# Start-up loads, five small products of the recurrent stage and the last group's sums rearranged in a hybrid attention and RWKV-7 block

## The chip, the cores and the metric

The kernel runs on one core of one Trainium2 chip. The metric is the device time of one execution in microseconds; several runs are timed and their median is given. One further execution is recorded by the hardware profiler, and all views of the profile come from it.

## The reference

One layer over 2048 rows of 1024 features, all in float32:

```python
h    = rms_norm(x, pre_mix_g)
proj = h @ w_in                     # 1536 attention, 1792 recurrent, 2048 gate columns
q, k, v = split(proj[:, :1536])     # 8 heads of 64: own chunk of 64 rows + 8 chunks before,
y_a  = softmax(q k^T / 8 + bias[distance]) v
p    = proj[:, 1536:3328]
p    = p + (previous row of p - p) * shift_mu
r, k, v, cw, ca, cg = split(p)      # 512, 512, 512, 64, 64, 128
decay = exp(-exp(-softplus(-(w0 + tanh(cw) @ w2)) - 0.5)); a = sigmoid(a0 + ca @ a2)
# per head, over time: state = state*decay + (state @ -kk) (kk*a)^T + v k^T;  y = state @ r
y_b  = (group_norm(y) + sum(r*k*r_k) * v) * (sigmoid(cg) @ g2)
m    = sigmoid(gA) * (y_a @ proj_a) + sigmoid(gB) * (y_b @ proj_b)
x    = x + rms_norm(m @ w_out, post_mix_g)
x    = x + rms_norm(relu(rms_norm(x, pre_ffn_g) @ w_up)**2 @ w_down, post_ffn_g)
```

## The kernel before

**Groups and products.** The rows are worked in four groups of 512 (`G`), each through a recurrent phase (`phase_rwkv`), an attention phase and a merge (`phase_merge`); the feed-forward part follows for two halves of the rows. A dense product of h with 128 columns of `w_in` (`dense`) splits the weight block into a high part `whi` (ScalarE, L70) and a low rest `wlo` (VectorE, L71) and forms 24 products of 128x128 by 128x512 (L80): for each of eight blocks of h high by high, the low half of h (`hl`) by `whi`, and `hh` by `wlo`. The raw weight, `whi` and `wlo` have two buffers each. Loads of weights and rows go out on SP's queue, in the queue's order; stores and the sums' transfers mostly on POOL's, gates' stores on ScalarE's.

**The start.** `phase_norm` loads the gain and four tiles of 128 rows; `norm_tile` squares each (L319, ScalarE), forms its root on POOL (`rstd`, L105 and L107), scales it (`xn`, L321, VectorE) and transposes it in eight products (L126), each half of which ScalarE copies to `hh` (L130) and VectorE reduces to `hl` (L131). Two PSUM tiles serve these transposes. Then come the constants: ten loads of rows (L203), four of w2 and a2 (L210), a transpose (L212) and small VectorE operations, the bias band (`build_bias`: `ext` loaded, extended on VectorE, stored as `band` at L961, then eight copies of it into `skew` in DRAM, L963) and eight copies that spread a small unit matrix into `x0` (L229). After that the group's projections start: block 12 for the low-rank inputs (`lora_wa`), then r, k, v of the first pair of heads. The low-rank products ps_z and ps_a (L360, L361) stand behind the second projection.

**The recurrent phase.** Four pairs of heads are prepared by `rwkv_pre`, which calls `between()` at eight places to let a gate's dense product, or steps of another pair's recurrence, run in. In it stand ps_ss and ps_v, the bonus product in two parts (ps_bonus from `rh` and `rl`, L488), and the scores ps_A (L517) in two halves of 16 products on two PSUM tiles each. All these small products share a pool of two PSUM tiles (`pa`). `rwkv_inverse` inverts 32x32 triangles for two pairs at a time on VectorE (X, turned at L560 and L562); `rwkv_blocks` completes them to 64x64 by 64 products ps_t of the turned X (L582), a copy Z (L585), and 64 more (L590). Then follow the transposes and products of `rwkv_trans`, the serial recurrence over eight chunks (L665 to L668), and `rwkv_post` (squares of ps_y, root, yn at L686).

**What sets the order.** An engine works off its own queue in order. The queue's order is fixed when the kernel is built, not by the program's text alone: the trace shows later dense products between small ones. `queue_behind` adds an order without a wait on data; before, `blocks_behind` places the first and the second 64 block products behind the 4th and 13th, or the 12th and 21st, product of a dense group of 24.

**The last group's merge.** While `phase_merge` forms ps_o (L1070) in two halves of the output columns, one of the kernel's sums of weight blocks runs beside it: four loads into the tile `cmb`, four subtractions on VectorE (L1121), four stores to `wd` on POOL's queue (L1145). It advances one step at k = 2, 4, 5, 6, 7 of the first half. The first half's results are squared (L1080, ScalarE) and scaled (L1081, VectorE), which frees PSUM for the second half. The feed-forward part's first operand is loaded into `bl` and split (`first_half`, `split_here`, L1158 and L1159). Its memory is that of tiles released before, `cmb` among them.

Of the kernel before, what the change touches and what calls it, by code (L numbers as in the profile page):

```python
# [18 lines left out]
P = 128  # L19
D = 1024  # L20
# [14 lines left out]
STEPS = (1, 2, 1, 1, 1, 1, 1, 1, 1, 1, 1, 0, 0, 2, 1)  # L35
DEC = math.exp(-0.5)
# [14 lines left out]
class Block:  # L51
# [6 lines left out]
    def wsplit(self, src, tag, k, n, raw_tag="raw", bufs=2):  # L58

        nc = self.nc  # L60
        w = self.wp
        raw = w.tile([P, k, n], F32, tag=raw_tag, name="wraw")
        nc.sync.dma_start(raw, src)
        hi = w.tile([P, k, n], F32R, tag=tag + "h", bufs=bufs, name="whi")
        lo = w.tile([P, k, n], F32R, tag=tag + "l", bufs=bufs, name="wlo")
        self.split(hi, lo, raw)
        return hi, lo

    def split(self, hi, lo, src):
        high = self.nc.scalar.copy(hi, src)  # L70
        self.nc.vector.tensor_tensor(lo, src, hi.bitcast(F32), ALU.subtract)  # L71
        return high.ins

    def mm3(self, ps, terms):
# [3 lines left out]
        for lh, ll, rh, rl in terms:  # L78
            for l, r in ((lh, rh), (lh, rl), (ll, rh)):
                mm.append(nc.tensor.matmul(ps, l, r, start=n == 0, stop=n == last).ins)  # L80
                n += 1
# [6 lines left out]
    def blocks_behind(self, *places):  # L88

        for ins, i in zip(self.blocks, places):  # L90
            self.queue_behind(ins, self.mm[i])

    def dense(self, col):

        wh, wl = self.wsplit(
            self.a["w_in"][:, col : col + P].rearrange("(k p) n -> p k n", p=P), "w", KB, P
        )
        ps = self.pd.tile([P, G], F32, tag="d", name="psd")
        self.mm = self.mm3(ps, [(wh[:, k], wl[:, k], self.h[0][:, k], self.h[1][:, k]) for k in range(KB)])
        return ps  # L100

    def rstd(self, pool, ssq, scale, eps, post=None):
        nc = self.nc
        v = pool.tile([P, 1], F32, tag="rs_v", bufs=4, name="rs_v")
        nc.gpsimd.tensor_scalar(v, ssq, scale, eps, ALU.mult, ALU.add)  # L105
        r = pool.tile([P, 1], F32, tag="rs_r", bufs=4, name="rs_r")
        nc.gpsimd.tensor_tensor(r, v, self.nhalf[:, 0:1], ALU.pow)  # L107
# [11 lines left out]
    def transpose_split(self, pt, src, hi, lo, tok, pinned=False):  # L119

        nc = self.nc
        for h in range(2):
            ps = pt.tile([P, 4, P], F32, tag="tr", name="pstr")
            for j in range(4):
                k = h * 4 + j
                mm = nc.tensor.transpose(ps[:, j], src[:, k * P : (k + 1) * P], self.ident)  # L126
                if pinned and j == 0:
                    self.tc.keep_in_program_order(mm)
            hv, lv = hi[:, h * 4 : h * 4 + 4, tok], lo[:, h * 4 : h * 4 + 4, tok]
            nc.scalar.copy(hv, ps)  # L130
            nc.vector.tensor_tensor(lv, ps, hv.bitcast(F32), ALU.subtract)  # L131


    def constants(self, ctx, mixing):
# [57 lines left out]
        with tc.tile_pool(name="setup", bufs=1, side="right") as sp, \  # L192
# [19 lines left out]
            nc.tensor.transpose(ps, raw, self.ident[:nrow, :nrow])  # L212
            nc.vector.tensor_copy(self.cst, ps)

            for par in range(2):
# [4 lines left out]
                nc.vector.tensor_tensor(  # L220
                    self.wl[par][r], raw2[par][r], self.wh[par][r].bitcast(F32), ALU.subtract
                )
            self.build_bias(sp, dp)
# [4 lines left out]
            for i in range(8):  # L228
                nc.sync.dma_start(  # L229
                    self.x0[i * 16 : i * 16 + 16].rearrange("p r j -> p (r j)"),  # L230
                    eyed[i % 2][None, :].to_broadcast((16, 512)),
                )
# [52 lines left out]
    def phase_norm(self, g, sp, pt, ahead=2):  # L285

        self.h = self.alloc_h()
        gt = self.gain(sp, self.a["pre_mix_g"], "g_pre", ahead if ahead == 2 else 1)
        for t in range(GT):
            x = sp.tile([P, D], F32, tag="x", bufs=ahead, name="x")  # L290
            self.nc.sync.dma_start(x, self.a["x"][g * G + t * P : g * G + (t + 1) * P])
            self.norm_tile(sp, pt, x, gt, *self.h, slice(t * P, (t + 1) * P), ahead)
            yield
# [21 lines left out]
    def norm_tile(self, sp, pt, x, gt, hi, lo, tok, ahead=2, pinned=False):  # L315
# [3 lines left out]
        nc.scalar.activation(xn, x, AF.Square, accum_out=ssq)  # L319
        r = self.rstd(sp, ssq, 1.0 / D, RMS_EPS)  # L320
        nc.vector.scalar_tensor_tensor(xn, x, r, gt, op0=ALU.mult, op1=ALU.mult)  # L321
        self.transpose_split(pt, xn, hi, lo, tok, pinned)

# [53 lines left out]
    def rwkv_pre(self, g, p, rp, NA, between=lambda: None):  # L377
# [13 lines left out]
        if p == 3:  # L391
            self.blocks_behind(3, 12)
# [94 lines left out]
        for i, x in enumerate((rh, rl)):  # L487
            nc.tensor.matmul(psb, self.bones, x, start=i == 0, stop=i == 1)  # L488
# [1020 lines left out]
```

## Time and profile before

| | |
|---|---|
| median of 3 runs | 3300.28 us (3299.59 to 3302.99) |
| profiled execution | 3302.74 us, span in the trace 3301.0 us |
| TensorE busy | 3189.4 us, 97% of the span |
| VectorE, ScalarE, POOL busy | 68%, 48%, 18% |
| DMA | 592.53 MB, mean 179 GB/s |

The page's first section gives each engine's busy time. A line of the waits reads: engine and line that waited, what it waited for, microseconds in total, number of times, the longest. A line of a timeline reads: start and length in us, engine, line of the kernel, operation, the tile written and the tiles read, sizes, number of instructions merged, and in brackets the idle time just before with what ended it. A stretch is a line with its bounds and length, the busy time and number of instructions of TensorE, its weight loads, VectorE, ScalarE and POOL, then the granted clock of TensorE, the share of the DMA engines and GB/s.

### The profile page before, as it was taken

To read this page: it belongs to the slowest core of one execution; us is meant where nothing else is said; L and a number is where in the kernel's file an instruction comes from. 1 tells how busy PE (TensorE), PEld (TensorE's weight loads), DVE (VectorE), ACT (ScalarE), POOL (GpSimd) and SP (SyncE) were. 2 spreads that over 40 slices of the span, in tenths; PEclk is the share of its full clock that TensorE was granted. 3 is DMA by queue.
4 is the path that set the end of the run, shared out by engine and by line. 5 is a ranking of instruction groups with operands and counts; after the bars stand their busy time and mean duration, and the time that the engine had idled before them with its cause. 6 is when DMAs were issued, how large, how long until landed. Compare 5 with 4: busy or idle time off the path is not lost. (4 is left out here: it accounts for less than half of the span.)

```text
span 3301.0 us, 49967 instructions
## 1 busy us (share of the span) xinstructions
PE 3189.4 (97%) x18913; PEld 2601.3 (79%) x18913; DVE 2245.6 (68%) x3655; ACT 1570.8 (48%) x2511; POOL 595.8 (18%) x1093
## 2 busy tenths in 40 slices
PE   7999999999999999999999999999999999999998
PEld 5777778778877777878777887878788878888887
DVE  5875766785766875776876775777656667775455
ACT  3434634434744434754444654544543454454343
POOL 2222012222102222111232110122211112220000
PEclk9999999999999999999999999999999999999999
DMA  5335473247564236555326647654787875546665
GB/s 152 90 110 185 129 239 118 81 131 240 170 223 150 87 108 222 189 194 185 96 76 201 200 155 234 231 179 153 248 291 239 285 248 190 170 161 235 193 215 178
DMA packets 432281, 592.53 MB, mean 179 GB/s; under 512 B 25300, under 2 KB 295840, under 8 KB 432040
## 3 DMA queue, kind: packets, MB, share of 16 engines
q1 hardware_dynamic: 375080, 413.14, 40.0%
q0 software_dynamic: 47744, 159.42, 13.1%
q10 hardware_dynamic: 9216, 16.78, 1.4%
q8 instruction: 149, 2.44, 0.3%
q14 instruction: 92, 0.75, 0.1%
HBM read 425.37 MB, written 167.01 MB: 179 GB/s over the span
## 5 line engine op out<-in xcount | busy, mean ns | idle before, releaser
L1345 PE MATMUL ps_dn<-fop 128*128 128x512 f32 x2688 | 611.8, 389 | 2.9 <-DVE fop L71 2.9
L1345 PEld LDWEIGHTS ps_dn<-fop 128*128 128x128 f32 x2688 | 503.9, 188 | 108.9 <-DVE fop L71 4.3
L80 PE MATMUL psd<-hh,whi 128*128 128x512 f32 x1344 | 541.4, 403 | 10.7 <-ACT whi L70 7.0
L80 PE MATMUL psd<-hl,whi 128*128 128x512 f32 x1344 | 542.4, 404 | 0.0
L80 PE MATMUL psd<-hh,wlo 128*128 128x512 f32 x1344 | 538.5, 401 | 2.6 <-DVE wlo L71 2.6
L70 ACT CAST whi<-wraw 128x1024 fp32r<-128x1024 f32 x232 | 243.3, 1049 | 424.1 <-PE psd L80 329.9
L71 DVE TENSOR_TENSOR wlo<-wraw,whi 128x1024 fp32r<-128x1024 f32 x232 | 282.9, 1220 | 165.9 <-ACT whi L70 139.1
L80 PEld LDWEIGHTS psd<-hh,whi 128*128 128x128 f32 x1344 | 255.9, 190 | 62.1 <-ACT whi L70 7.9
L80 PEld LDWEIGHTS psd<-hh,wlo 128*128 128x128 f32 x1344 | 256.1, 191 | 55.9 <-DVE wlo L71 5.1
L80 PEld LDWEIGHTS psd<-hl,whi 128*128 128x128 f32 x1344 | 256.5, 191 | 48.9
L71 DVE TENSOR_TENSOR fop<-xraw,fop 128x1024 fp32r<-128x1024 f32 x112 | 137.0, 1223 | 166.7 <-ACT fop L70 165.9
L70 ACT CAST fop<-xraw 128x1024 fp32r<-128x1024 f32 x112 | 117.8, 1052 | 244.9 <-PE ps_dn L1345 178.5
L1227 POOL DMA_DIRECT2D xd<-X x192 | 103.8, 541 | 394.3 <-ACT X L1224 339.5
L71 DVE TENSOR_TENSOR fop<-wdraw,fop 128x1024 fp32r<-128x1024 f32 x112 | 136.6, 1220 | 26.6 <-ACT fop L70 26.1
L70 ACT CAST fop<-wdraw 128x1024 fp32r<-128x1024 f32 x112 | 117.7, 1051 | 42.8 <-DMA wdraw<-in_w_down_dram 29.8
L903 DVE CUSTOM_DVE_ANT_0 sc<-bias,ps_s 128x640 f32<-128x640 f32 (+4 forms) x128 | 93.8, 732 | 54.0 <-PE ps_pt L914 32.2
L908 ACT ACTIVATE sc<-sc,mn 128x640 f32<-128x640 f32 (+4 forms) x128 | 97.7, 764 | 45.2 <-DVE mn L903 44.8
L70 ACT CAST s12h<-s 128x1024 fp32r<-128x1024 f32 x32 | 33.7, 1054 | 165.0 <-PE ps_u L80 165.0
L80 PE MATMUL ps_p<-yh,whi 128*128 128x512 f32 x256 | 101.3, 405 | 7.5 <-DVE th L1041 3.8
L1070 PE MATMUL ps_o<-whi,mh 128*128 128x512 f32 x256 | 101.6, 397 | 6.1 <-DVE o L1081 6.1
L919 DVE TENSOR_TENSOR PTl<-ps_pt,PTh 128x640 fp32r<-128x640 f32 (+4 forms) x128 | 94.2, 736 | 18.7 <-ACT PTh L918 17.2
L1070 PE MATMUL ps_o<-wlo,mh 128*128 128x512 f32 x256 | 100.6, 393 | 3.2 <-DVE wlo L71 3.2
(368 smaller groups left out, 6826.1 us busy)
## 6 DMA issues: line engine op xcount, KB each, us to landing
wraw<-in_w_in_dram SPq DMA_DIRECT2D x168, 512.0 KB
xraw<-xd SPq DMA_DIRECT2D x112, 512.0 KB
xd<-X POOLq DMA_DIRECT2D x192, 256.0 KB, 5.2
wraw<-in_w_up_dram SPq DMA_DIRECT2D x80, 512.0 KB
wdraw<-wd SPq DMA_DIRECT2D x64, 512.0 KB
wdraw<-in_w_down_dram SPq DMA_DIRECT2D x48, 512.0 KB
gd<-gate ACTq DMA_DIRECT2D x64, 256.0 KB
wd<-cmb POOLq DMA_DIRECT2D x64, 256.0 KB, 3.7
```

Source lines behind the costliest of these rows:

```text
L70: high = self.nc.scalar.copy(hi, src)
L71: self.nc.vector.tensor_tensor(lo, src, hi.bitcast(F32), ALU.subtract)
L80: mm.append(nc.tensor.matmul(ps, l, r, start=n == 0, stop=n == last).ins)
L903: nc.vector.tensor_tensor_reduce(sc[:, 0:n], bias[:, s0:640], pss[:, c0 : c0 + n], 1.0, 3.0e38, ALU.add, ALU.min, mn,)
L908: nc.scalar.activation(sc[:, 0:n], sc[:, 0:n], AF.Exp, scale=-1.0, bias=mn, accum_out=sm[:, col : col + 1])
L919: nc.vector.tensor_tensor(lv, pst[:, 0:nk], hv.bitcast(F32), ALU.subtract)
L1070: nc.tensor.matmul(ps[t], l[:, k, ts], r[:, k % 2], start=k == 0 and j == 0, stop=k == KB - 1 and j == 2)
L1227: nc.gpsimd.dma_start(self.xd[q][i // 2][:, i % 2], src)
L1345: nc.tensor.matmul(ps, o[:, l, k, sl], o[:, r, k], start=start and n == 0, stop=stop and n == end)
```

## The change

It has three parts.

The start: `first_norm` takes the place of `phase_norm`. The first tile of x is loaded ahead of the gain, and the raw weights of the first two projections (blocks 12 and 0) right behind the four tiles. Orders are added: each tile's root behind the one before it on POOL, tile 2's and 3's Square and scaling behind the copies of the tile two before, the two weights' high copies behind tiles 1 and 2, their low halves and the constants' operations on VectorE behind the last tile's low half, the constants' transpose and the first dense product behind the last tile's transposes. There are four PSUM tiles for the transposes. The first two projections form their 24 products by part: eight high by high, eight with `hl`, eight with `wlo`. The eight copies to `x0` and the eight to `skew` are no longer issued at the start but one at each `between()` of the first two calls of `rwkv_pre` in group 0 (`spread`).

The five small products: `dl` collects a group's dense products, and at the phase's end (`placed`) the second bonus part of pair 0, the first bonus part of pair 1, the first scores of pair 0, and the first and second block products are queued behind fixed positions of it. In the second recurrence two gates are given out at step 3 instead of one; their number stays 16.

The last group: the sums' tile moves to another place in memory, an unused tile lies in its old place, and the sums' steps come at k = 0, 2, 3, 4, 5.

```diff
+BLOCKS = ((412, 424), (623, 632))
+BONUS = {(0, 1): 138, (1, 0): 258}
+SCORES = 150
...
-    def wsplit(self, src, tag, k, n, raw_tag="raw", bufs=2):
+    def load_raw(self, src, k, n):
+        raw = self.wp.tile([P, k, n], F32, tag="raw", name="wraw")
+        self.nc.sync.dma_start(raw, src)
+        return raw
+
+    def wsplit(self, src, tag, k, n, bufs=2):
-        raw = w.tile([P, k, n], F32, tag=raw_tag, name="wraw")
-        nc.sync.dma_start(raw, src)
+        raw = self.raws.pop(0) if self.raws else self.load_raw(src, k, n)
...
+    def mm3(self, ps, terms, by_part=False):
-        for lh, ll, rh, rl in terms:
-            for l, r in ((lh, rh), (lh, rl), (ll, rh)):
-                mm.append(nc.tensor.matmul(ps, l, r, start=n == 0, stop=n == last).ins)
-                n += 1
+        pairs = [((lh, rh), (lh, rl), (ll, rh)) for lh, ll, rh, rl in terms]
+        for l, r in chain(*(zip(*pairs) if by_part else pairs)):
+            mm.append(nc.tensor.matmul(ps, l, r, start=n == 0, stop=n == last).ins)
+            n += 1
...
-    def blocks_behind(self, *places):
-        for ins, i in zip(self.blocks, places):
-            self.queue_behind(ins, self.mm[i])
+    def place(self, mm, n):
+        self.places.append((mm.ins, n))
+
+    def placed(self):
+        for ins, n in self.places:
+            self.queue_behind(ins, self.dl[n])
...
     def dense(self, col):
+        first = bool(self.raws)
+        wh, wl = self.wsplit(self.w_in(col), "w", KB, P)
+        if first:
+            self.queue_behind(self.high.ins, self.highs[2 - len(self.raws)])
+            self.queue_behind(self.low, self.last_low)
         ps = self.pd.tile([P, G], F32, tag="d", name="psd")
-        self.mm = self.mm3(ps, [(wh[:, k], wl[:, k], self.h[0][:, k], self.h[1][:, k]) for k in range(KB)])
+        self.mm = self.mm3(ps, [(wh[:, k], wl[:, k], self.h[0][:, k], self.h[1][:, k]) for k in range(KB)], first)
+        if first:
+            self.queue_behind(self.mm[0], self.last_transpose)
+        self.dl += self.mm
...
     def constants(self, ctx, mixing):
-            nc.tensor.transpose(ps, raw, self.ident[:nrow, :nrow])
-            nc.vector.tensor_copy(self.cst, ps)
+            self.queue_behind(nc.tensor.transpose(ps, raw, self.ident[:nrow, :nrow]).ins, self.last_transpose)
+            behind = lambda x: self.queue_behind(x.ins, self.last_low)
+            behind(nc.vector.tensor_copy(self.cst, ps))
...
+                behind(nc.vector.tensor_tensor(
                     self.wl[par][r], raw2[par][r], self.wh[par][r].bitcast(F32), ALU.subtract
+                ))
-            self.build_bias(sp, dp)
+            self.build_bias(sp, dp, behind)
...
-            for i in range(8):
-                nc.sync.dma_start(
-                    self.x0[i * 16 : i * 16 + 16].rearrange("p r j -> p (r j)"),
-                    eyed[i % 2][None, :].to_broadcast((16, 512)),
-                )
+            self.eyed = eyed
...
+    def first_norm(self, sp, pt):
+        self.h = self.alloc_h()
+        xs = []
+        for t in range(GT):
+            xs.append(sp.tile([P, D], F32, tag="x", bufs=GT, name="x"))
+            self.nc.sync.dma_start(xs[t], self.a["x"][t * P : (t + 1) * P])
+            if t == 0:
+                gt = self.gain(sp, self.a["pre_mix_g"], "g_pre")
+        self.raws = [self.load_raw(self.w_in(RW0 + blk * P), KB, P) for blk in (12, 0)]
+        steps = []
+        for t in range(GT):
+            steps.append(self.norm_tile(sp, pt, xs[t], gt, *self.h, slice(t * P, (t + 1) * P), GT))
+            square, root, scaled = steps[t][:3]
+            if t:
+                self.queue_behind(root[0], steps[t - 1][1][1])
+            if t > 1:
+                self.queue_behind(square, steps[t - 2][3])
+                self.queue_behind(scaled, steps[t - 2][4])
+        self.highs = [x[3] for x in steps]
...
     def rwkv_pre(self, g, p, rp, NA, between=lambda: None):
-        if p == 3:
-            self.blocks_behind(3, 12)
...
         for i, x in enumerate((rh, rl)):
-            nc.tensor.matmul(psb, self.bones, x, start=i == 0, stop=i == 1)
+            mm = nc.tensor.matmul(psb, self.bones, x, start=i == 0, stop=i == 1)
+            if (p, i) in BONUS:
+                self.place(mm, BONUS[p, i])
...
+                    if p == c == par == 0:
+                        self.place(mm, SCORES)
...
-    def rwkv_blocks(self, NA, Rs):
+    def rwkv_blocks(self, NA, Rs, b):
-        self.blocks = first[0], second[0]
+        for mm, n in zip((first[0], second[0]), BLOCKS[b]):
+            self.place(mm, n)
...
     def phase_rwkv(self, g, quads):
+            spread = self.spread() if g == 0 else iter(())
-                return lambda: act(next(it, 0))
+                def between():
+                    act(next(it, 0))
+                    advance(spread, 1)
+                return between
...
             Rs = [self.rwkv_pre(g, q, rp, NA, between) for q in range(2)]
+            advance(spread)
...
-                if i in (3, 9):
+                if i == 3:
+                    gate(2)
+                if i == 9:
                     gate()
-                if i == 3:
-                    self.blocks_behind(11, 20)
...
             gate(2 * KB)
+            self.placed()
...
+    def spread(self):
+        dma = self.nc.sync.dma_start
+        for i in range(8):
+            dma(
+                self.x0[i * 16 : i * 16 + 16].rearrange("p r j -> p (r j)"),
+                self.eyed[i % 2][None, :].to_broadcast((16, 512)),
+            )
+            yield
         for h in range(8):
-            nc.sync.dma_start(
-                self.skew[h].rearrange("(q m) -> q m", m=769)[:, 0:768], band[h][None, :].to_broadcast((P, 768))
+            dma(
+                self.skew[h].rearrange("(q m) -> q m", m=769)[:, 0:768],
+                self.band[h][None, :].to_broadcast((P, 768)),
             )
+            yield
...
     def phase_merge(self, g, o, op, between, beside):
-                    if n == 0 and k in (2, 4, 5, 6, 7):
+                    if n == 0 and k in ((2, 4, 5, 6, 7) if g + 1 < self.NG else (0, 2, 3, 4, 5)):
                         advance(beside, 1)
...
     def run(self):
-                 tc.tile_pool(name="p0p", bufs=2, space=PSUM, reuse_waits="tile") as pt:
-                advance(self.phase_norm(0, sp, pt, GT))
+                 tc.tile_pool(name="p0p", bufs=4, space=PSUM, reuse_waits="tile") as pt:
+                self.first_norm(sp, pt)
...
                     cmb = c.enter_context(tc.tile_pool(name="p1", bufs=1, reuse_waits="tile"))
+                    if g + 1 == self.NG:
+                        cmb.tile([P, 4 * G], F32, tag="pad", name="pad")
...
                     op = c.enter_context(tc.tile_pool(name="mo", bufs=1, reuse_waits="tile"))
+                    if g + 1 == self.NG:
+                        cmb = c.enter_context(tc.tile_pool(name="p2", bufs=1, reuse_waits="tile"))
```

48 lines of the change are left out of this document (21 added, 27 removed).

## Prediction

> **What bounds the kernel now.** I read the page's first lines, then the waits of TensorE, then the timeline and stretches of it at those waits.
>
> ```profile
> span 3301.0 us, 49967 instructions
> PE 3189.4 (97%) x18913; PEld 2601.3 (79%) x18913; DVE 2245.6 (68%) x3655; ACT 1570.8 (48%) x2511; POOL 595.8 (18%) x1093
> ...
> PE ps_t L582 <- DVE X L560: 9.6, 4, 2.4
> PE ps_t L590 <- ACT Z L585: 4.3, 8, 0.9
> PE ps_bonus L488 <- ACT rh L70: 4.0, 4, 1.0
> PE ps_bonus L488 <- DVE rl L71: 2.6, 7, 0.5
> PE ps_A L517 <- DVE BR L533: 2.5, 4, 0.6
> ```
>
> TensorE sets the time: only 111.6 us of its span are not busy, and no other engine passes 68%. The five lower lines (us in total, times, longest) are waits of the small products that the change moves; each wait that goes without a successor shortens the run by its length. A second loss hides inside "busy":
>
> ```profile
> 28.56 0.63 PE L80 MATMUL psd<-hl,whi 128*128 128x512 f32 x1
> 28.99 0.63 PE L80 MATMUL psd<-hh,wlo 128*128 128x512 f32 x1
> 36.77 0.39 PE L80 MATMUL psd<-hh,whi 128*128 128x512 f32 x1
> 36.99 0.39 PE L80 MATMUL psd<-hl,whi 128*128 128x512 f32 x1
> 156.00:162.00 6.00, 5.17 (x80) 3.98 (x82) 4.76 (x7) 4.13 (x9) 0.48 (x2) 0.72 0.18 54
> 254.00:258.00 4.00, 4.00 (x30) 2.97 (x32) 3.23 (x5) 2.39 (x4) 3.30 (x6) 0.59 0.58 177
> ```
>
> Early on, dense products start 0.43 us apart, later 0.22 to 0.23 (0.227 over long stretches): a slow one costs 0.2 more. The last two lines, stretches just after two of the waits above, show why: the granted clock (third number from the end) is 0.72 and 0.59 there. So a stall costs its length and a slow stretch behind it.
>
> **Part A, the start.**
>
> ```profile
> 6.72 1.06 ACT L319 ACTIVATE xn<-x 128x1024 f32<-128x1024 f32 x1 [4.65 <-DMA x<-in_x_dram]
> 8.04 1.06 ACT L319 ACTIVATE xn<-x 128x1024 f32<-128x1024 f32 x1 [0.16 <-DMA x<-in_x_dram]
> 9.04 1.28 DVE L321 SCALAR_TENSOR_TENSOR xn<-x,rs_r,g_pre 128x1024 f32<-128x1024 f32 x1 [3.66 <-POOL rs_r L107]
> 10.38 1.97 PE L126 MATMUL pstr<-ident,xn 128*128 128x128 f32 x8 [10.38 <-DVE xn L321]
> 11.64 0.57 ACT L130 CAST hh<-pstr 128x512 fp32r<-128x512 f32 x1
> 23.96 0.79 PE L80 MATMUL psd<-hh,whi 128*128 128x512 f32 x1 [1.62 <-ACT whi L70]
> 26.27 0.79 PE L80 MATMUL psd<-hh,wlo 128*128 128x512 f32 x1 [1.08 <-DVE wlo L71]
> 26.82 5.45 SPq L963 DMA_DIRECT2D skew<-band  x8
> 36.23 63.70 SPq L63 DMA_DIRECT2D wraw<-in_w_in_dram  x11
> 45.99 0.80 PE L80 MATMUL psd<-hh,whi 128*128 128x512 f32 x1 [5.41 <-ACT whi L70]
> ```
>
> The first product. Today the gain is loaded before the rows of x, and a 512 KB load takes 1.3 us (8.04 less 6.72). With the first rows in front of the gain they land at 5.4; the other three tiles stay at 8.0, 9.3 and 10.6, the two weights now issued next land near 11.9 and 13.2, and the 15 loads of constants queue behind those on SP. From a Square to its scaled xn are 2.3 us (6.72 to 9.04), the scaling takes 1.3, eight transposes 2.0, the copy of a high half 0.6. So tile 0 is transposed by 11.0 and copied by 11.6. Tile 2's Square, now queued behind that copy, starts at 11.6; tile 1 is copied by 14.1, where tile 3's Square starts; its xn runs from 16.4 to 17.7, its transposes to 19.7, its last copy to 20.3. First dense product at 20.3 instead of 23.96: **3.7 us**. Bounds: with tile 3 held by its load alone, 10.6 + 2.3 + 1.3 + 2.0 + 0.6 = 16.8, a gain of 7.2; where the added orders cost what they free, 0. I stay with the chain written out, between the two.
>
> The weights' low halves and the constants' small operations on VectorE move behind the last tile. What hides them is the new order of the first two projections: eight high-by-high products, eight with the low half of h, and only the 17th needs wlo. Sixteen products cover 3.6 us at 0.227 and 6.9 at 0.43; the clock is slow there today and I keep it so. The 1.08 us wait goes; with the cover gone (a fast clock, all constants in front) up to 2.5 us come back.
>
> The third projection. Its weights were issued at 36.23, behind eight skew copies of 384 KB; TensorE stood 5.41 us and then ran slow. The eight skew copies and eight small x0 copies now leave singly, one at each of 16 places of the two first pre-passes. What that frees is read from group 1, which has no such copies:
>
> ```profile
> 39.49 0.40 PE L360 MATMUL ps_z<-lora,whw 128*128 128x512 f32 x1
> 65.66 0.95 PE L421 MATMUL ps_ss<-bones,sq 128*128 128x2 f32 x8
> 529.22 0.47 PE L360 MATMUL ps_z<-lora,whw 128*128 128x512 f32 x1 [0.24 <-DVE lora L354]
> 546.58 0.95 PE L421 MATMUL ps_ss<-bones,sq 128*128 128x2 f32 x8
> ```
>
> From ps_z to ps_ss are 26.17 us against 17.36: **8.8 us**. SP can issue the third weights once wlo of the first projection is made (about 26), some 8 us before their product. Without that cover the 8.8 are paid again. Later the skew copies and the two masking copies behind them share SP and the DMA engines with eight weight loads; a weight is wanted once in 24 x 0.227 = 5.4 us and takes 1.3, a skew copy about 1, so there is room: nothing. A = 3.7 + 1.1 + 8.8 = **13.6**; bounds 3 (only what is sure of the first two terms) and 17.
>
> **Part B, five products in each of four groups.** I number a group's dense products from 0 by counting them in the timeline. The bonus products stand behind 134 (rl, first pair) and 252 (rh, second pair), the first scores behind 143, the blocks behind 411 and 420 (first inverse), 611 and 620 (second). They go behind 138, 258, 150, 412, 424, 623 and 632.
>
> ```profile
> 249.91 0.39 PE L80 MATMUL psd<-hh,wlo 128*128 128x512 f32 x1
> 252.69 1.20 PE L582 MATMUL ps_t<-X,NA 32*32 32x32 f32 x64 [2.39 <-DVE X L560]
> 257.66 1.20 PE L590 MATMUL ps_t<-XT,Z 32*32 32x32 f32 x64
> ...
> 255.63 1.18 ACT L585 COPY Z<-ps_t 32x512 f32<-32x512 f32 x2
> ...
> 252.53 1.18 DVE L71 TENSOR_TENSOR wlo<-wraw,whi 128x1024 fp32r<-128x1024 f32 x1
> ```
>
> Dense work put in front, against the wait in each group: rl 4 products (0.91 us) against 0.5; rh 6 (1.36) against 1.0; the blocks of the second inverse 12 (2.72) against 2.39; the second blocks of the first inverse 4 (0.91) against 4.3 / 4 = 1.1, of which I take 1.0. The score wait falls on the second half, eight products behind the first half, because VectorE comes late to the first; seven products (1.6 us) later it has caught up, if the second half moves along, as I take it to. Four groups: 2.0 + 4.0 + 9.6 + 4.0 + 2.5 = 22.1.
>
> Late next: the second blocks behind 632. Z is complete at 256.8 and hangs on VectorE and ScalarE, not on TensorE. TensorE now arrives at 249.9 + 13 x 0.227 + 1.2 + 9 x 0.227 = 256.1: a new wait of 0.6 to 0.7, four times, minus 2.6. The gate brought forward fills places 624 to 647; its low half is made at 252.53, in time for place 626 near 254.5.
>
> At the recurrence's end 12 fewer dense products remain:
>
> ```profile
> 291.77 0.28 PE L667 MATMUL ps_y<-ST,TQ 64*64 64x64 f32 x4
> ...
> 300.39 0.69 DVE L686 TENSOR_TENSOR yn<-ps_y,grs 128x512 f32<-128x512 f32 x1 [2.07 <-POOL grs L684]
> ```
>
> From the last ps_y to the second pair's yn are 9.3 us; before, 59 products (13.4 us) covered them, now 47 (10.7). Enough: nothing.
>
> The clock. From 252.69 + 1.2 to 257.66 nine products take 3.8 us, 2.0 at full rate: 1.7 more in each group, 6.8. Behind the wait near 156 (0.72) about four slow products, 0.8, in three groups: 2.4. What speaks for both going is the undelayed ps_t at 257.66, the nearest row: the same 64 small products without a wait in front, and the clock is full behind them. B = 22.1 - 2.6 + 9.2 = **28.7**. Bounds: 10 (the two ps_t waits net of the new one, no clock) and 33 (all, no new wait).
>
> The Trainium skill, "TensorE: Matmul & The Clock Gate", Part 1 (the HAM clock gate), says that the clock is halved only after an idle window of about 3.4 us. Here a wait of 2.39 us plus 1.2 us of 32x32 products was followed by 0.59, so the trace agrees only if such products count as idle. By that rule no window is left after the change, and B stays as summed; were the small products alone enough to halve it, B would be 19.5.
>
> **Part C, the last group.**
>
> ```profile
> 2015.18 0.54 POOL L1145 DMA_DIRECT2D wd<-cmb  x1 [0.19 <-issue]
> DMA to landing us min/median/max: 6.2/6.4/6.4
> 2021.65 0.34 SPq L1166 DMA_DIRECT2D bl<-ht  x1
> 2025.44 1.04 ACT L1158 CAST bh<-bl 128x1024 fp32r<-128x1024 f32 x1 [6.24 <-DMA bl<-ht]
> 2028.39 0.80 PE L1070 MATMUL ps_o<-whi,mh 128*128 128x512 f32 x1 [6.07 <-DVE o L1081]
> ```
>
> The last store of the sums, issued at 2015.18, lands 6.4 us later: the moment at which SP issues bl, whose memory it held. ACT stands 6.24 us at bh, the third eviction of ps_o is queued behind bh, and TensorE stands 6.07. After the change an unused pad lies in that place and the sums elsewhere; bl no longer waits for the store, bh starts near 2019.2, and the evictions behind it (a low half of 1.2 us on VectorE first) reach TensorE at about 2022.8 where it wants them at 2022.3. Gain 6.1 - 0.5, and 1.4 for the slow products behind the stall by the price above: **7.0**. The sums' loads also move up two steps on SP, ahead of a weight that is wanted 5.4 us later: nothing, at worst 1. Bounds 0 (the new place waits as long) and 7.5.
>
> **Sum.** 13.6 + 28.7 + 7.0 = 49.3. The profiled execution took 3302.74 us (its span and 1.74 around it), 2.46 above the median of the runs shown; 3302.7 - 49.3 = **3253**.
>
> **Rivals.**
> 1. The start's stall stays: SP is blocked at the band copy, which waits for VectorE's constants, now behind the last tile.
>
> ```profile
> SPq L961 <- DVE ext L960: 6.7, 1, 6.7
> ```
>
> It waits so today. Should it hold the third weights past their slack of 8 us, the 8.8 remain: 3262. Against it: those constants end near 26.
> 2. The small products' waits pass to their successors (Z, the banks of the two-buffer pool, the recurrence's end): half of B is lost, 3267.
> 3. bl stays late for another tile's sake: 3260.
> 4. The moved products keep their waits, since what they wait for moves too; A and C alone: 3282.
> 5. Slower: the dense product put in front of a small one is not there itself. Places 150 and 632 lie in a projection whose weights must be ready earlier than today; a miss costs what one cost at 45.99, 8.8. Eight places (two, four groups) give 3302.7 - 49.3 + 70 = 3324; from 49.3 / 8.8, six of the eight, it decides. Against it: the low half at 252.53 is early enough.
>
> **How the numbers follow.** My forecast 62% (own range 3243 to 3262), rival 1 12%, rival 2 15%, rival 3 5%, rival 4 3%, rival 5 3%. The range 3243 to 3276 has A at 17 and B at 33 at its low end and reaches past rival 2; rivals 4 and 5 stay outside. A measurement of this kernel tells about 0.2% (6.6 us) from no change; all cases but rival 5 are faster by more: 96%, same 1%, slower 3%.
>
> **What would show it.** Right: first dense product near 20.3, no idle before the 49th, 17.4 us from ps_z to ps_ss; the ps_t, ps_bonus and ps_A waits gone but for some 0.6 at L590; full clock behind ps_t; bl issued ahead of the sums' landing and no 6 us at ps_o. Wrong: a new wait of several us at the third projection's whi, at a gate inside the blocks, at the recurrence's end or at ps_o.

## The result and the profile after

The changed kernel takes 3275.01 us (median of four runs, 3272.42 to 3278.57); the kernel before took 3299.94 beside it (3299.13 to 3302.99). The ratio is 0.9915, 95% interval 0.9903 to 0.9928. That is 25 us faster, inside the range that was given (3243 to 3276) but half of the 49 us forecast. The profiled execution took 3273.41 us, 29.3 less than the one of before on which the sum was made.

The page's first lines after the change, the waits of TensorE (us in total, times, longest) in the recurrent stage and at the last group's output projection, and the rows of the start:

```profile
span 3271.7 us, 49957 instructions
PE 3178.6 (97%) x18913; PEld 2591.9 (79%) x18913; DVE 2244.4 (69%) x3655; ACT 1571.1 (48%) x2511; POOL 592.7 (18%) x1093
...
PE psd L88 <- ACT gate L747: 6.8, 8, 1.2
PE ps_at L643 <- ACT XT L628: 4.4, 4, 1.1
PE ps_st L699 <- DVE ST L702: 2.8, 4, 0.7
PE ps_bk L528 <- DVE BR L532: 2.7, 4, 0.7
PE ps_g L88 <- DVE yn L720: 2.3, 4, 0.6
PE ps_t L623 <- ACT Z L618: 2.2, 8, 0.4
PE ps_bonus L517 <- DVE rl L79: 2.0, 4, 0.5
PE ps_t L615 <- DVE X L593: 0.7, 4, 0.2
...
19.20 3.54 PE L88 MATMUL psd<-hh,whi 128*128 128x512 f32 x8
33.27 0.43 PE L391 MATMUL ps_z<-lora,whw 128*128 128x512 f32 x1
49.02 0.95 PE L450 MATMUL ps_ss<-bones,sq 128*128 128x2 f32 x8
```

The five waits shown before the change have shrunk: ps_t for X from 9.6 to 0.7, ps_t for Z from 4.3 to 2.2, and those for rh and of ps_A are not in the list any more. In their place stand psd for a gate's eviction, the copy that frees its PSUM tile (6.8 in all), ps_bk for BR, ps_g for yn, and ps_bonus for rl at another pair. The first three were not there before, and the fourth was under 0.2 us at that product. The wait of ps_at for XT has grown from 1.5 to 4.4.

Where the time went is read by taking the same product in both timelines and subtracting its starts. The first ps_ss of group 0 comes 16.64 us earlier (65.66 to 49.02): that is part A. In the four recurrent stages, each from its first ps_ss to its last ps_yt, 3.2, 3.4, 4.8 and 3.3 us are gained, 14.7 in all. The last group's merge, up to the first product of the feed-forward stage, gains 3.6. Together 34.9; the stretches between the recurrent stages (attention and merge of groups 0 to 2) gave 4.8 back in this execution, the feed-forward stage 0.9. Such starts of the same product are called landmarks below.

### The profile page after: what moved, and what is told of

Read it like the earlier page. It is cut to its first block, busy times and chain, and to the rows that moved or that the text cites. A ratio compares the mean times of both kernels' runs of the same rounds, so it can differ in the third digit from the quotient of the medians.

```text
span 3271.7 us, 49957 instructions
## 1 busy us (share of the span) xinstructions
PE 3178.6 (97%) x18913; PEld 2591.9 (79%) x18913; DVE 2244.4 (69%) x3655; ACT 1571.1 (48%) x2511; POOL 592.7 (18%) x1093
## 3 DMA queue, kind: packets, MB, share of 16 engines
q0 software_dynamic: 47744, 159.42, 13.3%
## 5 line engine op out<-in xcount | busy, mean ns | idle before, releaser
L88 PE MATMUL psd<-hl,whi 128*128 128x512 f32 x1344 | 533.1, 398 | 0.0
L88 PE MATMUL psd<-hh,wlo 128*128 128x512 f32 x1344 | 531.2, 397 | 0.0
```

## The experiments

The runs come in three series: e1 to e4, e5 to e8 and e9 to e12. Each time is set against the kernel before in the same series, since its median moved between them (3303.0, 3300.2, 3300.6 us). The intervals of the ratios reach 4 to 5 us to either side, so medians do not tell apart smaller differences; for these the waits and the landmarks of the profiles are used.

**Which part gave what.** Four kernels take parts of the change away.

```diff
e1  -BLOCKS = ((412, 424), (623, 632)); BONUS = {(0, 1): 138, (1, 0): 258}; SCORES = 150
    +BLOCKS = ((411, 420), (611, 620)); BONUS = {}          # and gate() at 3 and 9
e2  -cmb.tile([P, 4 * G], F32, tag="pad", name="pad")        # last group: pad and pool p2
    -(2, 4, 5, 6, 7) if g + 1 < self.NG else (0, 2, 3, 4, 5)
    +(2, 4, 5, 6, 7)
e3  both edits
e4  only the second edit of e2 (pad and p2 stay)
```

> The five products and the gate stand where they stood before the change; the start and the last group stay changed. Theory 1 (in the recurrent stage the waits passed to the next product of TensorE's queue, so that part B is worth only what the landmarks of the two traces show, about 10 us in four groups, whatever the other parts do): 3280 to 3286 us, and the recurrent stage of group 1, from its first ps_z to its last ps_yt, is 3 to 4 us longer than after the change. Theory 2 (part B is worth its forecast 28.7, and the rest of the change loses the difference): 3297 to 3304. Also open: the wait of 2.55 us for KK in group 0's attention; if it comes from the start (part A) it stays here, if it comes from part B it goes.

> The last group's sums lie in memory and are loaded as before the change; the rest stays changed. Theory 1 (part C is worth the 3.6 us that the landmarks show, since 6 us go at ps_o and about 3 come back as waits of ps_o and ps_p for weights behind the sums' loads): 3277 to 3280 us, with one wait of about 6 us at ps_o and none at whi or wlo there. Theory 2 (part C is worth its forecast 7.0, and the new waits would be there without it): 3281 to 3283.

> Only the start is changed. By the landmarks the start is worth 16.7 us: 3283 to 3287 us. Theory 1 (the parts add up): its distance to e1_without_B is 2 to 5 us and to e2_without_C 7 to 12. Theory 2 (what one part frees, another takes): one of the two distances is under 1 or over 20.

> All of the change, but the last group's loads of sums stand at the old steps 2, 4, 5, 6, 7 of the output projection. Theory 1 (the loads at steps 0, 2, 3, 4, 5 stand ahead of the output weights on SP's queue, and that makes the new waits of ps_o for whi and wlo, 0.8 and 0.95 us, the slow products behind them, some 1.6, and perhaps the wait of ps_p for th, 1.2 more than before): 3270 to 3273 us, and those waits are gone. Theory 2 (the waits come from the moved memory, not from the steps): 3274 to 3276, waits as they are. Theory 3 (the steps are needed, as the sums come late without them): 3277 to 3280, with a new wait for the sums.

| kernel | median us | below before | ratio, 95% interval |
|---|---|---|---|
| e1, A and C | 3283.84 | 19.2 | 0.9949, 0.9935 to 0.9963 |
| e2, A and B | 3274.88 | 28.2 | 0.9924, 0.9910 to 0.9937 |
| e3, A | 3286.32 | 16.7 | 0.9951, 0.9937 to 0.9965 |
| e4, all, old load steps | 3270.84 | 32.2 | 0.9905, 0.9889 to 0.9921 |

So A is worth 16.7, B 11.4 on top of it (e3 to e2; in the profiles the four recurrent stages are 13.3 us shorter), and C as it was made about nothing that these medians can tell. Theory 1 held for the times of e1 and e3 (e1's group 1, from ps_z on, is 2.3 us longer than after the change, where 3 to 4 were expected). For e2 its waits came as expected (6.2 us at ps_o, none at whi), its time did not: 3274.88 is below the 3277 to 3280 that theory 1 gave, so that C was worth less than the 3.6 of the landmarks. e4 is 4.0 below e2, less than the medians tell apart; in the profiles its stretch from the last recurrent stage to the feed-forward stage is 5.4 us shorter. That is what the new memory place is worth once the loads stand at their old steps. The rows of TensorE at the output projection, first after the change, then e4, then e2:

```profile
1963.04 0.50 PE L88 MATMUL ps_p<-yh,whi 128*128 128x512 f32 x1 [1.50 <-DVE th L1097]
1989.20 0.50 PE L1126 MATMUL ps_o<-whi,mh 128*128 128x512 f32 x1 [0.83 <-ACT whi L78]
1990.65 0.50 PE L1126 MATMUL ps_o<-wlo,mh 128*128 128x512 f32 x1 [0.95 <-DVE wlo L79]
```

```profile
1959.28 0.50 PE L88 MATMUL ps_p<-yh,whi 128*128 128x512 f32 x1 [1.54 <-DVE th L1097]
1991.10 0.50 PE L1126 MATMUL ps_o<-whi,mh 128*128 128x512 f32 x1 [1.60 <-DVE o L1137]
```

```profile
1997.96 0.80 PE L1126 MATMUL ps_o<-whi,mh 128*128 128x512 f32 x1 [6.24 <-DVE o L1137]
```

The waits for whi and wlo come with the new steps (theory 1): none of the nine kernels with the old steps shows one there. But the new steps do not always bring them; e1, which has these steps too, has neither, and e5 only 0.2 us for wlo. The wait of ps_p for th comes with the new memory (theory 2 for that one): all eleven kernels that have it wait there for 1.5 to 3.8 us, the three others (before, e2, e3) for 0.34 at most. In e4 the last merge from ps_p's end to ps_o's end is 6.2 us shorter than before, after the change 3.6. The wait for KK in group 0's attention (2.55 us after the change) does not belong to the start: e1 and e3 have none. e2 has 1.5 us of it and e4, with the same products up to there, none, so that it hangs on the execution as well. The 4.8 us given back between the recurrent stages are no lasting part of the change either: e1, e2 and e4 gain 1.6, 1.1 and 2.7 there.

**Which move in part B.** On A and C, one kind of move at a time.

```diff
e5  BLOCKS = ((412, 424), (623, 632)), gate(2) at 3;  BONUS = {}, no SCORES
e6  BONUS = {(0, 1): 138, (1, 0): 258};  BLOCKS old, gates old, no SCORES
e7  SCORES = 150;  BLOCKS old, gates old, BONUS = {}
```

> The start and the last group stay changed; of the recurrent stage only the blocks of the two inverses (412, 424, 623, 632) and the gate brought forward are moved, bonus products and scores stand at their old places. From its profile, waits of TensorE in the recurrent stages, four groups, against e1_without_B (35.4 us): Theory 1 (dense products are a fixed stock of cover, so that those put ahead of the blocks are missing behind them): ps_t's waits fall from 14.2 to about 3, and the waits of psd for a gate's eviction (6.8) and of ps_g for yn (2.3) appear here already; in all 6 to 8 us less wait, and 3275 to 3280 us. Theory 2 (the blocks' own gain is kept, the new waits come from the bonus products and scores): no psd wait for a gate, 12 to 15 us less wait, 3268 to 3272.

> The start and the last group stay changed; of the recurrent stage only the two bonus products are moved (138 and 258). Theory 1 (the wait passes to the next product of the queue where the moved product holds one of the two banks, and to the low half that stands right behind it): ps_bonus for rh falls from 4.0 to 0 and rl of the first pair goes (2.7), but ps_bk for BR appears with 2.7 and ps_bonus for rl of the second pair with 2.0: 2 us less wait in four groups, 3280 to 3284 us. Theory 2 (the forecast: each wait goes without a successor): 6 us less, 3276 to 3279.

> The start and the last group stay changed; of the recurrent stage only the first pair's scores are moved (150). Theory 1 and the forecast: ps_A's wait for BR (2.6 in four groups) goes and nothing takes its place: 3280 to 3283 us. Rival (the scores free their banks later, so that the next pair's products wait): the stage's waits stay at 35 us, 3283 to 3286.

They took 3277.26 (23.0 below before), 3285.72 (14.5) and 3286.46 us (13.8), against 19.2 for e1 in the series before. e6 and e7 are slower than every range given for them, by 2 us and less than 1 us. e5's recurrent stages have 27.2 us of waits against 35.4 in e1 and 24.7 after the change, and they are 10.7 us shorter than e1's: the blocks are nearly all of B (after the change: 12.9 shorter), and the waits for the gate (6.7) and for yn (2.3) come with them, as theory 1 said. e7's wait of ps_A (2.6) goes and no wait replaces it; its stages are 2.2 us shorter than e1's, as much as forecast, which its median does not show. e6 is the telling one. Its waits of ps_t, ps_bk and ps_bonus:

```profile
PE ps_t L613 <- DVE X L591: 11.2, 8, 2.4
PE ps_t L621 <- ACT Z L616: 4.3, 8, 0.7
PE ps_bk L528 <- DVE BR L532: 2.7, 4, 0.7
PE ps_bonus L517 <- DVE rl L79: 2.0, 4, 0.5
```

The waits for rh (4.0 in e1) and for rl of the first pair (2.7) are gone. ps_bk and the second pair's rl took 4.7 of them over, and the rest is paid at ps_t, whose wait for X rises from 9.5 to 11.2. Nothing is gained: the stages are 4.2 us longer than e1's, with more slow products. My 6 us were not there.

**Moving the successors too.** From here on all kernels have the old load steps (e4).

```diff
e8  +place(second ps_bk of pair 0, 140); BONUS +(1, 1): 261; +place(second ps_at of the first inverse, 433)
e9   e4 with BLOCKS = ((411, 420), (623, 632))
e10  e8 with BLOCKS = ((416, 428), (634, 643)) and the second ps_at at 437
e11  e8 with nc.gpsimd.tensor_tensor(AR[:, :, 2], r3, E[:, :, 1 : C + 1], ALU.mult)   # was nc.vector
e12  e10 and e11
```

> All of the change with the old load steps (e4), and the three products that took over a wait put behind denser ones too: the second ps_bk of the first pair behind product 140, rl of the second pair behind 261, the second ps_at of the first inverse behind 433. In four groups they wait 2.7, 2.0 and 4.4 us in e4, whose stages have 24.7 us of waits. Theory 1 (fixed stock of cover): bk and rl go, since dense products are plentiful there, but the 4.4 of ps_at come back as waits of psd, ps_st or ps_g in the recurrence behind it: 19 to 21 us of waits, 3265 to 3268 us. Theory 2 (a wait only passes to the next product each time): 23 to 25 us of waits, 3269 to 3273. Theory 3 (three places were simply missing): 15 to 17 us, 3260 to 3264.

> All of the change with the old load steps (e4, 32.2 us below the kernel before in its call), but the blocks of the first inverse stand at their old places (411, 420); those of the second stay at 623 and 632. In every kernel so far the recurrence behind the first inverse begins behind dense product 455, so that four products put ahead of the blocks are taken from the 35 behind them. Theory 1 (fixed stock): the waits of psd for a gate's eviction fall from 6.8 to about 2.1 and those of ps_t for Z rise from 2.2 to about 4; the stages' waits are 22 to 26 us (24.7 in e4), the time 29 to 35 us below before. Theory 2 (the forecast: the move is a gain of 4.0 by itself): waits 28 to 30, the time 26 to 29 us below before.

> As e8, with the blocks still later (416, 428, 634, 643) and the second ps_at behind 437, since in e8 ps_t waits 12.9 us for X again. Theory 1 (the waits only change their place): ps_t's wait for X falls under 3, but ps_st, ps_ug, psd and ps_yt rise by as much; the stages' waits stay at 25 to 29 us (28.6 in e8) and the time at 29 to 34 us below before. Theory 3 (only the places were wrong): waits 16 to 19, the time 38 to 43 us below before.

> As e8, and VectorE is relieved: the product of r and E in each pair's preparation (0.69 us each, four in a group) runs on GpSimd. Theory 1 (VectorE's chain sets when X is ready, so that what TensorE saves ahead of the blocks is given back there): X is ready about 1.2 us earlier in each half, ps_t's wait for X falls from 12.9 to 4 to 8 us, and the time is 35 to 39 us below before (e8: 31.2). Theory 2 (X is held by something else, or GpSimd's slower product, some 1.3 us, is late for the scores): wait for X as it is or new waits of ps_A, 27 to 32 us below before.

> Both edits of e10 and e11. If the places alone were wrong, as e10 (38 to 43 us below before). If VectorE's chain holds TensorE in the recurrence as well (ps_st waits for ST, ps_ug for WA), the relief shows here as a gain of 2 to 6 us over e10. If cover is a fixed stock, 31 to 36 us below before.

| kernel | median us | below before | waits in the four stages, us |
|---|---|---|---|
| e8 | 3269.05 | 31.2 | 28.6 |
| e9 | 3278.39 | 22.3 | 30.2 |
| e10 | 3259.23 | 41.4 | 19.6 |
| e11 | 3274.63 | 26.0 | 27.9 |
| e12 | 3268.03 | 32.6 | 20.1 |

In e8 the three waits went, 8 of 9 us, and the wait for X came back at both blocks (12.9); the time did not move (31.2 against e4's 32.2). I had three theories on record, and none had X in it; the time is that of theory 2, in which a wait only passes to the next product, the waits are above all three. e9 and e10 then decided against theory 1 of e8, that dense products are a fixed stock and cover no more than they uncover elsewhere. Taking four of them from before the first blocks makes the kernel slower (e9: 22.3 below before, e4 32.2, in different series; the intervals just overlap, and the four stages are 6.2 us longer in the profiles). Neither of e9's two ranges for the time held. Putting more in front of the blocks makes the kernel 10.2 us faster (e10 against e8). e10 is the fastest kernel of this study: ratio to before 0.9873, interval 0.9860 to 0.9886. e11 and e12, meant to relieve VectorE, took 5 and 9 us longer than e8 and e10; for e11 the intervals overlap. e12's time lies where I had put the fixed stock, 31 to 36 below before, but its waits are those of e10.

The rows that explain it are the second blocks of group 1: their start, and the start of the stage (ps_ss), in before, after, e6, e8 and e10, in this order (ps_ss of before, 546.58, stands in the prediction).

```profile
733.75 1.20 PE L582 MATMUL ps_t<-X,NA 32*32 32x32 f32 x64 [2.39 <-DVE X L560]
```

```profile
529.91 0.95 PE L450 MATMUL ps_ss<-bones,sq 128*128 128x2 f32 x8
686.32 2.04 DVE L574 STREAM_TRANSPOSE N<-NA 128x1024 f32<-128x1024 f32 x1
693.07 0.69 DVE L720 TENSOR_TENSOR yn<-ps_y,grs 128x512 f32<-128x512 f32 x1 [1.68 <-POOL grs L718]
714.01 1.15 DVE L593 STREAM_TRANSPOSE X<-X 128x512 f32<-128x512 f32 x1
716.23 1.20 PE L615 MATMUL ps_t<-X,NA 32*32 32x32 f32 x64
```

```profile
530.15 0.95 PE L450 MATMUL ps_ss<-bones,sq 128*128 128x2 f32 x8
717.43 1.85 PE L613 MATMUL ps_t<-X,NA 32*32 32x32 f32 x64 [2.42 <-DVE X L591]
```

```profile
528.92 0.95 PE L450 MATMUL ps_ss<-bones,sq 128*128 128x2 f32 x8
714.28 1.06 DVE L595 STREAM_TRANSPOSE X<-X 128x512 f32<-128x512 f32 x1
715.39 1.21 PE L617 MATMUL ps_t<-X,NA 32*32 32x32 f32 x64 [2.35 <-DVE X L595]
```

```profile
523.99 0.95 PE L450 MATMUL ps_ss<-bones,sq 128*128 128x2 f32 x8
708.28 1.16 DVE L595 STREAM_TRANSPOSE X<-X 128x512 f32<-128x512 f32 x1
709.51 1.20 PE L617 MATMUL ps_t<-X,NA 32*32 32x32 f32 x64
```

From ps_ss to the second blocks are 187.17, 186.32, 187.28, 186.47 and 185.52 us. X, which the blocks need, is ready at 185.3 to 187.2 us of the stage in these five. Only after the change TensorE comes clearly later than X, by 1.1 us (716.23 less 714.01 and 1.15), since its own queue ahead has new waits.

What holds X can be read on VectorE. Its second inverse begins with N (156.4 us into the stage after the change), and from there to X's end VectorE works through its own queue for 28.8 to 30.1 us of group 1 in all fourteen kernels, waiting 1.7 to 2.0 us in all, for a root from GpSimd. It does not wait for TensorE there, so that from N on its own queue sets X. N itself comes 1.7 us earlier after the change than before (158.1), and in e8 as early; but in e8 one more weight's low half (1.2 us) stands between N and X, and X is ready 1.2 us later than after the change.

What differs is how many dense products are done by the time of the blocks: 611, 623, 611, 623 and 634. The eleven of e10 over e8 are 11 x 0.227 = 2.5 us in group 1, and its blocks start 0.95 us earlier in their stage: 3.4 of gain, as measured (241.31 to 237.89). The four stages of e10 are 12.5 us shorter than e8's; the medians differ by 10.2.

## Why the prediction was half right

The time lay inside the range that was given, but only 1 us from its upper end, which had been set to reach past rival 2; the forecast of 3253 and its own range, 3243 to 3262, were missed. That the whole was not further off is partly luck: part A gave 3 us more than forecast, while B and C together gave half of their 35.7 (18.3 by the landmarks).

**The view and the bound** held: TensorE set the time in every kernel, and its short waits were where the time lay.

**Part A**, 13.6 forecast, 16.7 measured (e3), 16.64 in the profile. The first product came at 19.20 instead of the 20.3 written out, 4.8 earlier than before. From ps_z to ps_ss are 15.75 us, not the 17.36 borrowed from group 1. Its mechanism was right; its three terms measured 4.8, 1.5 and 10.4 where 3.7, 1.1 and 8.8 were forecast. Rival 1, the stall that stays, did not happen.

**Part B** is where the sum failed, and the step has a name: "each wait that goes without a successor shortens the run by its length", applied to five waits of one queue as if they were independent, 22.1 in all. Added up over the four stages, the five waits shrank by 18.1, but others grew or came by 14.7 where 2.6 had been set (psd for the gate 6.8, ps_at for XT 2.9, ps_bk for BR 2.7, ps_g for yn 2.3). With some smaller ones that went, TensorE's waits fell from 32.0 to 24.7, by 7.3 and not by 19.5. One of the new ones stands where the prediction wrote "Enough: nothing", at the recurrence's end: 0.6 a group for yn. Rival 2 had this mechanism ("the small products' waits pass to their successors"), with half of B lost: by the landmarks B lost 14.0 of 28.7, by the medians 17.3. Two bounds of B and the low end of the range do not come out of their own terms: with all waits gone and no new one it is 31.3, not 33, and the two waits of ps_t less the new one are 11.0, not 10; and 3302.7 less 17, 33 and 7.5 is 3245, not 3243.

Group 1, the bracketed waits of TensorE's timeline added up, in us, and the dense products of over 0.6 us:

| | before | after | e8 | e10 |
|---|---|---|---|---|
| ahead of the first blocks | 2.29 | 1.16 | 0 | 0 |
| from the first blocks to the second | 3.10 | 3.67 | 4.10 | 2.91 |
| second blocks for X | 2.39 | 0 | 2.35 | 0 |
| behind the second blocks | 0 | 1.30 | 0.58 | 1.76 |
| slow products | 12 | 0 | 7 | 0 |
| stage, ps_ss to last ps_yt | 244.04 | 240.66 | 241.31 | 237.89 |

(The second line has the first blocks' own wait for X in it: 0.18 after the change, 0.82 in e8.) After the change the rows behind this are:

```profile
537.25 0.66 PE L528 MATMUL ps_bk<-ident,BK 128*128 128x128 f32 x4 [0.67 <-DVE BR L532]
573.51 0.50 PE L517 MATMUL ps_bonus<-rl,bones 128*128 128x512 f32 x1 [0.49 <-DVE rl L79]
...
624.88 0.66 PE L643 MATMUL ps_at<-ident,AR 128*128 128x128 f32 x4 [1.09 <-ACT XT L628]
...
670.91 0.50 PE L88 MATMUL psd<-hh,whi 128*128 128x512 f32 x1 [1.17 <-ACT gate L747]
...
717.95 0.50 PE L88 MATMUL psd<-hh,whi 128*128 128x512 f32 x1 [0.52 <-ACT gate L747]
...
767.97 0.70 PE L88 MATMUL ps_g<-lora_g,g2h 128*128 128x512 f32 x2 [0.58 <-DVE yn L720]
```

The moved rl, now at 538.22, leaves the bonus product half done and its PSUM tile taken, one of two; meanwhile the second ps_bk, at place 136, waits 0.67 for the eviction of the first. rl of the second pair stands right behind the moved rh and waits 0.49 for its low half. At 670.91 a dense product waits 1.17 for ScalarE to evict a gate: on ScalarE that gate stands behind a whi cast which itself waited 1.19 for TensorE:

```profile
669.09 1.05 ACT L78 CAST whi<-wraw 128x1024 fp32r<-128x1024 f32 x1 [1.19 <-PE psd L88]
670.17 0.69 ACT L747 ACTIVATE gate<-psd,hgb 128x512 f32<-128x512 f32 x1
```

e5 shows that this one comes with the blocks.

Each of these is a product that TensorE now reaches before its operand. e8 shows what happens when they are moved as well: TensorE is early at the blocks instead. e6 showed it first. The 3.1 us of waits ahead of the second blocks (0.5, 1.0, 0.6 and 1.0 by my terms) could not be gained beside the 2.4 at X, for X does not come earlier by as much: with them gone, the twelve products put in front were no longer enough. I had set 2.72 against 2.39, which holds only if TensorE otherwise arrives when it did. Counted in dense products, the gain is what is put in front until X is there, 12 x 0.227 = 2.72, and the 0.85 by which the second blocks start earlier in their stage: 3.57, less 0.2 lost behind them, 3.38 measured in group 1. The forecast was 7.2.

That the first inverse's move pays by itself, which I took at 1.0 a group, is borne out in part: e9 has 5.5 us more wait than e4, with ps_t's wait for Z at 9.8 against 2.2. Of these 7.6 us only 2.8 stand at the first inverse, 0.7 a group; the rest stands at the second, whose places e9 had not changed, and why is open.

**The clock term**, 9.2, was right in size for the slow products, but not all of it was gained. In the four stages of before 43 dense products took over 0.6 us, after the change none; at 0.2 each 8.6. Twelve of them stood behind the first inverse's blocks, four each in groups 0, 1 and 3, the 2.4 of the forecast. Behind these stands ps_at, which waits for XT from ScalarE. These are its rows of before in group 1, where the four slow products stand ahead of it, and in group 2, where none does:

```profile
641.85 1.12 PE L609 MATMUL ps_at<-ident,AR 128*128 128x128 f32 x4 [0.20 <-ACT XT L594]
1151.67 0.55 PE L609 MATMUL ps_at<-ident,AR 128*128 128x128 f32 x3 [1.11 <-ACT XT L594]
```

After the change all four groups wait 1.1 us: the slow products had only filled that wait, and their 2.4 came back in it. With the waits' 7.3 the slow products' 8.6 make 15.9, against the 14.7 by which the stages got shorter. A stretch just behind the second blocks, e8's of groups 0 and 1, then that of group 0 after the change (granted clock third from the end):

```profile
236.69:240.69 4.00, 4.00 (x32) 3.26 (x27) 2.63 (x4) 3.53 (x6) 3.12 (x6) 0.50 0.37 105
716.70:720.70 4.00, 4.00 (x32) 2.96 (x34) 2.63 (x4) 3.54 (x6) 3.14 (x6) 0.60 0.37 93
```

```profile
236.70:240.70 4.00, 3.41 (x67) 2.65 (x69) 3.49 (x5) 3.23 (x5) 3.04 (x5) 1.00 0.73 187
```

**Part C**, 7.0 forecast, 3.6 in the profile and nothing clear in the medians. The stall of 6.07 us did go. The step that failed is "nothing, at worst 1" for the sums' loads: two steps earlier on SP they cost TensorE 0.83 and 0.95 us of waiting for the output weights and the slow products behind, 2.6 us between e4 and the change at that place. And freeing bl early had a price that I did not look for: its cast, bh, now stands in ScalarE's queue within the merge, where ScalarE waits 2.73 us for bl's load; VectorE waits 1.41 behind it, and TensorE 1.50 at ps_p for th:

```profile
1959.48 1.05 ACT L1214 CAST bh<-bl 128x1024 fp32r<-128x1024 f32 x1 [2.73 <-DMA bl<-ht]
...
1960.56 1.23 DVE L1215 TENSOR_TENSOR bl<-bl,bh 128x1024 fp32r<-128x1024 f32 x1 [1.41 <-ACT bh L1214]
```

**Rivals 3 to 5** did not happen: bl was early, the moved products lost their waits, and no dense product ahead of a moved one missed its weights.

## What to carry to other kernels

Waits of one in-order queue that stand ahead of the same event of another engine are not added up. Mark the events that the other engine sets (here X, some 29 us of VectorE's queue behind N), and count how much useful work stands in front of each; a wait that ends before such an event pays only if there is more work to put in front of it. After moving one product, read who stands behind it and what it holds (a PSUM tile, a half-finished sum), and move that too, then fill the wait that comes up: here the first round gave 11 us, the second nothing and the third 10.

## What the runs showed that I had not expected

The slow clock behind a short wait is a matter of chance, not of certainty. In six kernels (before, e1, e3, e6, e7 and e8) ps_t waited for X at the second blocks: 24 waits of 2.35 to 2.43 us, each followed by 1.2 us of 32x32 products. Dense products of over 0.6 us followed in 20 cases and not in 4; behind four waits of 1.85 to 1.87 us (e11) in one case. In the four kernels with the blocks at 623 and 632 and those of the first inverse at 412 and 424 (after, e2, e4, e5), the same products without the wait were followed by slow ones in none of 16; in e9 and e10, where the second ps_t waits 0.8 to 1.0 us for Z there, in 4 of 8. At the first blocks of e11 waits of 1.2 us were followed by slow products in one group of four, to a granted clock of 0.57 from 1627.8 to 1631.8:

```profile
1626.69 1.20 PE L617 MATMUL ps_t<-X,NA 32*32 32x32 f32 x64 [1.19 <-DVE X L595]
1628.94 0.63 PE L88 MATMUL psd<-hh,wlo 128*128 128x512 f32 x1
```

The Trainium skill, "TensorE: Matmul & The Clock Gate", Part 1, describes an activity window of about 3.4 us that runs freely. The waits of 2.4 us with the 1.2 us of small products behind them, 3.6 in all, agree with it if small products count as idle. The wait of 1.19 us does not: with its small products it makes 2.4, so that here less than a whole idle window was sometimes enough.

Work taken from VectorE and given to GpSimd did not relieve VectorE. In e11 sixteen products of 0.69 us went to GpSimd, 11.0 us, and VectorE's busy time fell by 3.7 us (2243.3 in e8, 2239.6). The rest came back as slower operations while GpSimd ran, nine of them by 7.7 us in all. Two of these, with an operation of the same line without GpSimd:

```profile
600.13 1.16 DVE L592 TENSOR_TENSOR X<-X,T 128x121 f32<-128x121 f32 x1
655.47 0.74 DVE L365 SCALAR_TENSOR_TENSOR k<-pr,cst,k 128x512 f32<-128x512 f32 x1
...
658.95 1.69 DVE L365 SCALAR_TENSOR_TENSOR v<-pr,cst,v 128x512 f32<-128x512 f32 x1
```

```profile
658.29 1.80 POOL L480 TENSOR_TENSOR AR<-r,E 128x512 f32<-128x512 f32 x1 [0.53 <-ACT E L436]
```

Line 365 takes 0.74 us alone and 1.69 beside GpSimd's product, line 592 1.16 where a step of that size takes 0.3. That one is a step of X's own chain in the first inverse, slowed once in each group, so that e11 is no clean test of what a relieved VectorE would do for X; X was ready at 186.5 us of the stage, as in e8. The Trainium skill, "GPSIMD Engine Reference", section 1 (Specifications), says that GpSimd shares its SBUF interfaces with VectorE and that VectorE instructions with two SBUF inputs contend for them; the trace agrees, with the 1.69 against 0.74 us above.

Where e11 and e12 lost their time is open. It is not where the moved products run: e11's four recurrent stages are 1.8 us shorter than e8's, e12's 0.6 longer than e10's. The stretch from the last recurrent stage to the feed-forward stage is 7.4 and 5.3 us longer, with longer waits of ps_p and more slow products, and no run here tells that from chance.
